# Splitting the next stage's weights piece by piece inside the last block of a two-layer hybrid decoder step, and parting the last two output tiles by columns

## The chip, the cores and the metric

The kernel runs on one core of a Trainium2 chip. The metric is the device time of one execution in microseconds (us), smaller being better. In the profile PE is the matrix engine TensorE, DVE is VectorE, ACT is ScalarE, POOL is GpSimd, and SP is the engine whose queue issues nearly all the transfers here.

## The reference, cut to what matters

The computation is one inference step of a decoder of DEPTH = 2 layers over 2048 prompt rows, 16 meta rows and 8 sample rows, all in fp32, with a width of 1024. Each layer is

```python
proj = einsum('btd,de->bte', rms_norm(h), w_in[l])      # one combined input projection
# its columns are split to four head groups: a (HGRN2), b (gated DeltaNet), c (Mamba-2 SSD), d (retention)
b_conv = causal_conv(b_qkv, gdn_ctx, gdn_conv_w)        # width 4, then silu
c_conv = causal_conv(c_xbc, ssd_ctx, ssd_conv_w, ssd_conv_b)
# each group: a recurrence over chunks of rows, a norm, a gate
y = concatenate([y_a, y_b, y_c, y_d], axis=-1)
h = h + einsum('bte,ed->btd', y, w_out[l])
```

and a last rms_norm follows the second layer. The recurrent states after the prompt and after the samples are outputs too.

## The kernel before

**Tiles and stages.** The 2072 rows are 17 row tiles: tile 0 has 40 rows (meta, samples and padding), the others 128. They make 8 blocks: block 0 is tiles 0 to 2, the others two tiles each. In each layer the kernel runs five stages over all the blocks: C, B, A, D (one head group each: its dense products, convolution, recurrence), then `outproj`, which for each tile multiplies by `w_out`, adds to `h`, stores it, normalizes it and prepares the next layer's input (`xprep`: a row norm, transposes on PE at L518, a high part by ACT at L523 and a low part by DVE at L524, stores to `xh` and `xl`).

**Products.** Each fp32 product is three matmuls over a high and a low part (high by high, low by high, high by low): L484 to L486 for `dense_cm` (columns of the weights on the partitions of the result, up to 296 rows of the block at a time), L494 to L496 for `dense_tm` and `dense_rows` (rows of the block on the partitions). The results land in `pd`, of which there are two buffers.

**Weights.** A piece of weights (128x1024 fp32, 512 KB) is loaded by SP into a buffer `wr` from a pool of five (`f4`), which other tiles share; then ACT casts it to the high part `wh` (L458) and POOL or DVE subtracts that to get the low part `wl` (L459). `wpiece` does all three. Which engine subtracts is set by `lopool[0]`, from the numbers `PC0` (C of layer 0), `PC1` (C of layer 1), `PB`, `PA`, `PD`: 1 is POOL, 0 is DVE, 2 is both in turn. C has row pieces with a small rest `wn` beside (one buffer) and six convolution pieces; B has six convolution pieces (q, k, v in two halves each) and two gate pieces (z); A has eight.

**Order.** The code is written in Python and a scheduler orders the instructions of each engine by a simulated time line; each engine's queue and SP's then run strictly in that order. `early()` raises the priority of what is written inside it. So the weights of the next stage are asked for in one go at its head, in the order that the scheduler finds.

**Convolution.** `conv` (L924) computes six groups of 128 columns. Each takes 24 matmuls into one `pd`, and then four taps: ACT takes the first from `pd` (L953 for C, L955 for B; in block 0 from copies `u`, L943 to L945), DVE adds three (L957) and keeps three columns of history (`hC`, `hB`, L959), ACT takes a tanh (L961) and DVE multiplies (L962). In C, each tile's recurrence begins with PE's `tr<-cc,cb`, and needs `cgu`, which POOL makes by a select (L1417) in a buffer of the W2 pool. POOL's L1534 is a part of the sample rows' recurrence. Beside B's convolution, a chain `walkB` over chunks goes from PE (`wo`, `tr`) through DVE (L313, L1264) and POOL. SP's L1151, L1188 and L1190 belong to its preparation, as do POOL's own transfers `bU` and `bR` (L1161, L1162).

**Between layers.** At tile 16 of layer 0's `outproj`, the next layer's C weights are asked for between its two column halves (`between`).

Of the kernel before, what the change touches and what calls it, by code (L numbers as in the profile page):

```python
# [93 lines left out]
def body(tc, ctx, a, o, nch, depth, blks, off):  # L94
# [87 lines left out]
    PC0, PC1, PB, PA, PD, PO = 1, 1, 1, 2, 0, 0  # L182
# [8 lines left out]
    WEARLY = 1  # L191
# [246 lines left out]
    def wpiece(src, nd, n, wide=False):  # L438
        raw = f4([128, 1024], "wr")
        hi, lo = (wp.tile([128, 4 * 268 if wide else 1024], F32R, tag=("v" if wide else "w") + x, bufs=2 if wide else 6,  # L440
                          name="w" + x) for x in "hl")
        hv, lv = (x[:, 0:nd * n].rearrange("p (d e) -> p d e", d=nd) for x in (hi, lo))
# [5 lines left out]
        for s in src:  # L448
            w = s.shape[1]
            r, c0, c1 = parts[c >= m]  # L450
            nc.sync.dma_start(r.rearrange("p (d e) -> p d e", d=nd)[:, :, c - c0:c - c0 + w],
                              s.rearrange("(o p) e -> p o e", p=128))
            c += w
        on_pool = lopool[0] == 1 or lopool[0] > 1 and (lopool[0] + lopool[1]) % 2
# [5 lines left out]
        return hv, lv  # L460

# [246 lines left out]
    def weightsA(w):  # L708
        return ([load_cm(w, A_Q + 128 * p) for p in range(2)], [load_cm(w, A_F + 128 * p) for p in range(2)],
                load_tm(w, [(A_I, 256)]), [load_cm(w, A_Z + 128 * p, True) for p in range(2)])  # L710

    def mixA(L, W, b):
        wq, wff, wi, wz = W
# [210 lines left out]
    def conv(L, ws, b, wi, key, hasb, out):  # L924
# [10 lines left out]
        for i in range(6):  # L935
# [3 lines left out]
            def ev(ps):  # L939
# [10 lines left out]
                for (src, u0, n, yc) in parts:  # L950
# [60 lines left out]
    def weightsB(w):  # L1011
        return [load_cm(w, B_QKV + 128 * i) for i in range(6)], [load_cm(w, B_Z + 128 * p, True) for p in range(2)]

    def denseB(L, W, b):
        b.qkv = [blk("b" + c) for c in "qkv"]
        conv(L, W[0], b, 0, "B", False, b.qkv)
        z = blk("z")
        for p in range(2):
            dense_cm(W[1][p], b, lambda ps: silu2(ps, z[:, p, 0:b.n], b.n))
            hook(rB)  # L1020
        nc.sync.dma_start(zdr[b.i], z[:, :, 0:b.n])
# [375 lines left out]
    def mixC(L, W, b):  # L1397
# [25 lines left out]
        conv(L, W[1], b, 6, "C", True, xbc)  # L1423
# [238 lines left out]
    def outproj(L, W, t, Ln, between=None):  # L1662
# [3 lines left out]
        yh, yl = xpair((NT - t) % 2, 128)  # L1666
# [4 lines left out]
        for qd in range(2):  # L1671
# [3 lines left out]
            if between:  # L1675
                with early():
                    next(between)
                    Wn = next(between)
        if Ln is not None:
            nc.sync.dma_start(hdr[t], hx[0:R])  # L1680
            xprep(Ln, t, hx)
            if between:
                return Wn
        else:
# [3 lines left out]
            else:  # L1688
                nc.sync.dma_start(o["y_prompt"][0, 128 * (t - 1):128 * t, :], hx)

# [19 lines left out]
    nblk = len(blocks)  # L1710
    ld = load_layer(0)
    Ln = next(ld)
    for l in range(depth):
# [24 lines left out]
        walk.append(walkB(L))  # L1738
        for i in range(-1, nblk, 2):
            bs = blocks[max(i, 0):i + 2]  # L1740
            for b in bs:
                if not b.last:
                    load_x(blocks[b.i + 1])
                denseB(L, W, b)
# [6 lines left out]
            if WEARLY and bs[-1].last:  # L1751
                lopool[0] = PA
                with early():
                    W = weightsA(w)
# [11 lines left out]
        for weights, mix in ((weightsA, mixA), (weightsD, mixD)):  # L1766
            if not (WEARLY and weights is weightsA):
# [80 lines left out]
```

## Time and profile before

| | |
|---|---|
| time, median of 3 runs (lowest to highest) | 2859.1 us (2859.03 to 2863.05) |
| the profiled execution: time, span | 2864.64 us, 2862.9 us |
| mean granted TensorE clock | 0.982 of full |
| busy: PE, DVE, ACT, POOL | 95%, 60%, 36%, 37% |
| stages, layer 0 (ends, about) | C 328, B 614, A 1050, D 1255, outproj 1462 us |
| stages, layer 1 (ends, about) | C 1746, B 2021, A 2455, D 2660, outproj 2863 us |

The profile records for every instruction its start, its duration and, in brackets, how long its engine stood idle before it and what ended that. Times count from the start of the span. The granted clock is a share of 2.4 GHz, so that 0.5 is 1.2 GHz. A mean of 0.8 in a stretch means that the lower level held for 0.4 of it.

### The profile page before, as it was taken

To read this page: it belongs to the slowest core of one execution; us is meant where nothing else is said; L and a number is where in the kernel's file an instruction comes from. 1 tells how busy PE (TensorE), PEld (TensorE's weight loads), DVE (VectorE), ACT (ScalarE), POOL (GpSimd) and SP (SyncE) were. 2 spreads that over 40 slices of the span, in tenths; PEclk is the share of its full clock that TensorE was granted. 3 is DMA by queue.
4 is the path that set the end of the run, shared out by engine and by line. 5 is a ranking of instruction groups with operands and counts; after the bars stand their busy time and mean duration, and the time that the engine had idled before them with its cause. 6 is when DMAs were issued, how large, how long until landed. Compare 5 with 4: busy or idle time off the path is not lost.

```text
span 2862.9 us, 66636 instructions
## 1 busy us (share of the span) xinstructions
PE 2713.3 (95%) x26372; PEld 2463.7 (86%) x26372; DVE 1704.0 (60%) x4864; ACT 1034.1 (36%) x2601; POOL 1065.6 (37%) x2032
## 2 busy tenths in 40 slices
PE   6999999989999899999989999999999999999998
PEld 6889898989889788888778999888898887888787
DVE  5777765657656655454346767656676667445533
ACT  4545532333434422232244445223443443222321
POOL 4454545557323221110033535555773322211100
PEclk9999999999999999999999999999999999999999
DMA  7243445563321423236672433544632323331443
GB/s 179 67 142 110 147 128 139 149 173 102 98 74 61 150 77 113 77 112 204 211 231 80 127 108 119 141 121 134 184 82 90 88 83 114 98 108 67 139 140 111
DMA packets 385152, 349.31 MB, mean 122 GB/s; under 512 B 144312, under 2 KB 349616, under 8 KB 374600
## 3 DMA queue, kind: packets, MB, share of 16 engines
q1 hardware_dynamic: 381320, 335.95, 38.8%
q0 software_dynamic: 3520, 9.09, 1.7%
q8 instruction: 209, 3.42, 0.5%
q14 instruction: 103, 0.84, 0.1%
HBM read 247.05 MB, written 98.10 MB: 121 GB/s over the span
## 4 chain that ended last, share of the span: by engine, by line
PE 74%; DVE 8%; DMA 7%; POOL 4%; ACT 3%; issue 3%; SPq 1%; POOLq 0%; ACTq 0%; DVEq 0%
PE pd L494 10%; PE pd L496 9%; PE pd L495 9%; PE pd L484 9%; PE pd L485 8%; PE pd L486 8%; PE tr L236 7%; PE wo L236 4%; PE sc L236 4%; PE o L236 3%; DMA wr<-in_w_in_dram 3%; PE tr L622 1%; ACT wh L458 1%; PE tr L518 1%; POOL bR L1168 1%
## 5 line engine op out<-in xcount | busy, mean ns | idle before, releaser
L484 PE MATMUL pd<-xh,wh 128*128 128x256 f32 (+1 forms) x2816 | 828.4, 294 | 34.7 <-DVE hB L959 11.5
L486 PE MATMUL pd<-xh,wl 128*128 128x256 f32 (+1 forms) x2816 | 814.8, 289 | 0.6 <-DVE wl L459 0.6
L485 PE MATMUL pd<-xl,wh 128*128 128x256 f32 (+1 forms) x2816 | 815.3, 290 | 0.0
L484 PEld LDWEIGHTS pd<-xh,wh 128*128 128x128 f32 x2816 | 542.7, 193 | 56.9 <-issue 20.0
L494 PE MATMUL pd<-wh,xh 128*128 128x512 f32 (+5 forms) x1632 | 563.1, 346 | 7.4 <-DVE sraw L1406 4.4
L495 PE MATMUL pd<-wl,xh 128*128 128x512 f32 (+5 forms) x1632 | 558.2, 342 | 5.1 <-POOL wl L459 4.4
L496 PE MATMUL pd<-wh,xl 128*128 128x512 f32 (+5 forms) x1632 | 558.2, 342 | 0.0
L486 PEld LDWEIGHTS pd<-xh,wl 128*128 128x128 f32 x2816 | 542.8, 193 | 5.2 <-issue 3.2
L485 PEld LDWEIGHTS pd<-xl,wh 128*128 128x128 f32 x2816 | 542.9, 193 | 3.1 <-issue 1.3
L494 PEld LDWEIGHTS pd<-wh,xh 128*128 128x128 f32 (+1 forms) x1632 | 304.1, 186 | 45.7 <-issue 4.6
L495 PEld LDWEIGHTS pd<-wl,xh 128*128 128x128 f32 (+1 forms) x1632 | 304.4, 187 | 41.6 <-POOL wl L459 5.0
L496 PEld LDWEIGHTS pd<-wh,xl 128*128 128x128 f32 (+1 forms) x1632 | 304.0, 186 | 38.6 <-issue 1.7
L313 DVE TENSOR_TENSOR sbd<-low,tr 64x128 f32<-64x128 f32 x384 | 109.0, 284 | 130.0 <-PE tr L236 116.1
L336 POOL TENSOR_TENSOR fm<-fm,expo 128x4 f32<-128x4 f32 (+3 forms) x136 | 131.1, 964 | 80.0 <-DVE fm L613 72.6
L611 POOL TENSOR_SCALAR fm<-fm 128x4 f32<-128x4 f32 (+3 forms) x102 | 25.0, 245 | 352.1 <-DVE fm L608 325.4
L340 POOL TENSOR_SCALAR rm<-rm 128x1 f32<-128x1 f32 (+1 forms) x51 | 14.0, 275 | 353.5 <-ACT junk L358 352.5
L244 POOL COPY bwi<-wz 32x256 f32<-32x256 f32 x128 | 59.8, 467 | 206.7 <-DVE wz L1264 203.7
L531 ACT ACTIVATE th<-pd 128x256 f32<-128x256 f32 (+2 forms) x162 | 62.5, 386 | 187.4 <-PE pd L486 143.5
L1168 POOL TENSOR_TENSOR bR<-bR,bW 128x120 f32<-128x120 f32 (+14 forms) x300 | 119.0, 397 | 21.0
L1167 POOL TENSOR_TENSOR bW<-bU,bR 128x120 f32<-128x120 f32 (+14 forms) x300 | 112.8, 376 | 33.2 <-DMA bR<-bscr 12.8
L1674 DVE TENSOR_TENSOR hx<-hx,pd 128x512 f32<-128x512 f32 (+1 forms) x68 | 46.6, 686 | 119.9 <-PE pd L496 118.5
L513 DVE SCALAR_TENSOR_TENSOR hx<-hx,rm,sq 128x512 f32<-128x512 f32 (+1 forms) x68 | 53.1, 819 | 104.5 <-POOL rm L336 103.5
(531 smaller groups left out, 5135.6 us busy)
## 6 DMA issues: line engine op xcount, KB each, us to landing
xh<-xh SPq DMA_DIRECT2D x56, 1024.0 KB
xl<-xl SPq DMA_DIRECT2D x56, 1024.0 KB
wr<-in_w_in_dram SPq DMA_DIRECT2D x64, 512.0 KB
hx<-in_x_prompt_dram SPq DMA_DIRECT2D x32, 512.0 KB
y<-y SPq DMA_DIRECT2D x128, 128.0 KB
yf<-y SPq DMA_DIRECT2D x32, 512.0 KB
bld<-qkv SPq DMA_DIRECT2D x32, 384.0 KB
xh<-xh SPq DMA_DIRECT2D x8, 1184.0 KB
```

Source lines behind the costliest of these rows:

```text
L236: T.matmul(out, l, r, start=start, stop=stop, skip_group_check=True)
L313: tt(new[rr, :, hh], low[rr, :, hh], pv, ALU.add)
L336: G.tensor_tensor(dst, src, e.broadcast_to(list(src.shape)), ALU.pow)
L484: T.matmul(ps, hi[:, d], b.xh[:, d, 0:b.n], start=(d == 0), stop=False)
L485: T.matmul(ps, hi[:, d], b.xl[:, d, 0:b.n], start=False, stop=False)
L486: T.matmul(ps, lo[:, d], b.xh[:, d, 0:b.n], start=False, stop=(d == 7))
L494: T.matmul(ps[0:R, 0:n], xh[:, d], hi, start=(d == 0), stop=False)
L495: T.matmul(ps[0:R, 0:n], xh[:, d], lo, start=False, stop=False)
L496: T.matmul(ps[0:R, 0:n], xl[:, d], hi, start=False, stop=(d == 7))
L531: act(th[0:R, 0:n], ps, AF.Tanh, scale=0.5)
L1167: f(wv, bcm(U_[0:2 * nu, j, j + 1:32], 1, m), bcl(R_[0:2 * nu, 0:m, j], 31 - j), ALU.mult)
L1168: f(R_[0:2 * nu, 0:m, j + 1:32], R_[0:2 * nu, 0:m, j + 1:32], wv, ALU.subtract)
```

## The change

1. `PC0` and `PC1` become 0: the low parts of C's weights are computed by DVE and no longer by POOL, in both layers.
2. `wpiece` is parted into `wraw` (the transfer) and `wsplit` (cast and subtract). A generator `staged` keeps transfers two pieces ahead and does one split for each `next`, kept in written order on ACT, DVE and POOL.
3. In the last block of C, B's weights are fed so: one `next` after each of the six groups of `conv`. In the last block of B, A's are, after each of the six groups and the two gate products. `arrived` does what is left.
4. In layer 0's first block of C only the first two convolution pieces are asked for ahead; the other four come one by one inside `conv` (`more`).
5. `outproj` becomes a generator. Between the layers tiles 15 and 16 are done by column halves: both tiles' first half, C's row pieces, both tiles' second half, C's other pieces. Their row end (the store of `h` and `xprep`) is put off until after block 0 of the next layer's C (`tails`).
6. `cgu` of tile 0 moves from the W2 pool to an own small buffer (the tag `bma`).

```diff
-    PC0, PC1, PB, PA, PD, PO = 1, 1, 1, 2, 0, 0
+    PC0, PC1, PB, PA, PD, PO = 0, 0, 1, 2, 0, 0
...
+    def staged(pieces):
+        raws, out = [], []
+        for k, pc in enumerate(pieces):
+            while len(raws) < min(k + 2, len(pieces)):
+                raws.append(wraw(*pieces[len(raws)][0:3]))
+            yield None
+            with inorder((ET.Activation, ET.DVE, ET.Pool)):
+                out.append(wsplit(raws[k], *pc[1:]))
+        yield out
+    coming = []
+    def feed():
+        if coming:
+            coming[1] = next(coming[0], None) or coming[1]
+    def arrived():
+        while coming[1] is None:
+            feed()
+        out = coming[1]
+        coming.clear()
+        return out
...
-    def conv(L, ws, b, wi, key, hasb, out):
+    def conv(L, ws, b, wi, key, hasb, out, more=None):
...
+            if more:
+                with inorder((ET.Activation, ET.DVE)):
+                    next(more, 0)
             dense_cm(ws[i], b, ev, True)
             hook(rB)
+            if b.last:
+                feed()
...
-                gu = w2([128, 4, 128], "cgu", F32R)
+                gu = w2([128, 4, 128], "cgu", F32R) if t else k2.tile([128, 4, 32], F32R, tag="bma", bufs=2, name="cgu")
...
-            W = list(weightsC(w))[-1]
+            more = weightsC(w)
+            W = [next(more) for _ in range(2)][-1]
...
         for b in blocks:
             if not b.last:
                 nextx(blocks[b.i + 1])
-            mixC(L, W, b)
-            if not b.first:
+            else:
+                lopool[0] = PB
+                coming[:] = weightsB(w), None
+            mixC(L, W, b, more if l == 0 and b.first else None)
+            if b.first:
+                for x in tails:
+                    next(x)
+            else:
                 decode(L)
         decode(L, True)
-        lopool[0] = PB
-        with early():
-            W = weightsB(w)
         load_x(blocks[0])
+        W = arrived()
...
+                else:
+                    lopool[0] = PA
+                    coming[:] = weightsA(w), None
                 denseB(L, W, b)
...
-            if WEARLY and bs[-1].last:
-                lopool[0] = PA
-                with early():
-                    W = weightsA(w)
+            if bs[-1].last:
+                W = arrived()
...
-        for t in range(NT):
-            if t == NT - 1 and Ln is not None:
-                lopool[0] = PC1
-                parts = weightsC(a["w_in"][l + 1])
-                W = outproj(L, W, t, Ln, parts)
-            else:
-                outproj(L, W, t, Ln)
+        tails = []
+        for t in range(NT if Ln is None else NT - 2):
+            for _ in outproj(L, W, t, Ln):
+                pass
+        if Ln is not None:
+            lopool[0] = PC1
+            parts = weightsC(a["w_in"][l + 1])
+            both = xpair(1, 256)
+            tails = [outproj(L, W, NT - 2 + k, Ln, [x[:, :, 128 * k:128 * k + 128] for x in both]) for k in range(2)]
+            for _ in range(2):
+                for x in tails:
+                    next(x)
+                with early():
+                    next(parts)
+                    W = next(parts)
```

The lines after it have other numbers: L449 is before's L451, L463 is L458, L991 is L955, L997 is L961, L1460 is L1417, L1577 is L1534.

**POOL between the layers.** In the queue before stand the low parts of C's weights, then the sample rows' L1534, then `cgu`:

```order
L459 TENSOR_TENSOR wl<-wr,wh 128x1024
L459 TENSOR_TENSOR wl<-wn,wh 128x4x12
L336 TENSOR_TENSOR rm<-rm,expo 128x1
L459 TENSOR_TENSOR wl<-wr,wh 128x1024 x4
L340 TENSOR_SCALAR rm<-rm 128x1
L336 TENSOR_TENSOR rm<-rm,expo 128x1
L1765 MEMSET sq_114 128x512
L1765 MEMSET sq_115 128x512
L1534 TENSOR_TENSOR dcS<-dcS,dce 128x1024
L1417 AFFINE_SELECT cgu<-gh 32x4x32 x2
L1417 AFFINE_SELECT cgu<-gh 128x512 x2
```

and now:

```order
L340 TENSOR_SCALAR rm<-rm 128x1
L336 TENSOR_TENSOR rm<-rm,expo 128x1
L1460 AFFINE_SELECT cgu<-gh 32x128 x2
L1577 TENSOR_TENSOR dcS<-dcS,dce 128x1024
L1460 AFFINE_SELECT cgu<-gh 128x512 x2
```

The weights have left this queue, and `cgu` of tile 0 (`32x...`) stands ahead of the sample rows' step, that of tile 1 still behind it.

**ACT where B ends and A begins, layer 1.** `bv` are the last two groups of the last block's convolution (the first piece of a group is L955, its tanh L961), and `wh<-wr` are casts of A's weights. Before:

```order
L961 ACTIVATE th<-bv 128x256
L955 ACTIVATE bv<-pd,cwh 128x256
L961 ACTIVATE th<-bv 128x256
L1273 COPY boq<-wo 32x256
L531 ACTIVATE th<-pd 128x256
L458 CAST wh<-wr 128x1024
```

and now:

```order
L991 ACTIVATE bv<-pd,cwh 128x256
L1316 COPY boq<-wo 32x256
L463 CAST wh<-wr 128x1024
L997 ACTIVATE th<-bv 128x256
L463 CAST wh<-wr 128x1024 x2
L991 ACTIVATE bv<-pd,cwh 128x256
L306 ACTIVATE low<-sbd_113,bEG 128x128 x2
```

Three casts stand ahead of the last group's first tap, where none did. In layer 0 two casts stood there before (L458 x2 ahead of the second L955), and three do now.

**SP at the start of layer 0.** `wr<-in_w_in_dram 128x8x128` is a convolution piece of C, `hx` an input tile, `xh_135` the store of the prepared block 0. Before:

```order
L451 DMA wr<-in_w_in_dram 128x8x128
L380 DMA cwt<-in_gdn_conv_w_dram 128x6x1
L382 DMA cwt<-in_ssd_conv_w_dram 128x6x1
L387 DMA cb<-in_ssd_conv_b_dram 128x6x1
L451 DMA wr<-in_w_in_dram 128x8x128 x2
L1699 DMA xh_135<-xh 128x2368
L1699 DMA xl_143<-xl 128x2368
```

and now:

```order
L1739 DMA xh_135<-xh 128x2368
L395 DMA smc<-in_ssd_d_dram 128x4
L405 DMA lg<-in_hgrn_lb_logits_dram 128x2x1
L1739 DMA xl_143<-xl 128x2368
L405 DMA lg<-in_hgrn_lb_logits_dram 128x2x1
L350 DMA hx<-in_x_prompt_dram 128x1024 x2
L970 DMA cx<-in_state_ssd_conv_dram 24x256 x3
L449 DMA wr<-in_w_in_dram 128x8x128 x3
```

Three of the six convolution pieces have moved behind the stores of block 0 and two input tiles of block 1; the sixth comes later still.

## Rows read from the trace of the kernel before

**Rows 1.** The page, part 1: busy time, share of the span, instructions.
```profile
PE 2713.3 (95%) x26372; PEld 2463.7 (86%) x26372; DVE 1704.0 (60%) x4864; ACT 1034.1 (36%) x2601; POOL 1065.6 (37%) x2032
```

**Rows 2.** Table by stretch; the last three columns are granted clock, DMA share, GB/s.
```profile
core 0: us, PE busy (x) PEld busy (x) DVE busy (x) ACT busy (x) POOL busy (x), PEclk, DMA share, GB/s
328.00:340.00 12.00, 7.63 (x46) 7.22 (x45) 9.14 (x20) 3.25 (x13) 6.39 (x5) 0.86 0.25 106
595.00:610.00 15.00, 5.96 (x44) 5.41 (x43) 6.45 (x15) 4.97 (x9) 5.85 (x8) 0.79 0.98 207
1462.50:1519.20 56.70, 42.36 (x269) 40.77 (x267) 30.22 (x87) 26.21 (x68) 21.94 (x18) 0.82 0.67 187
...
1502.00:1505.00 3.00, 3.00 (x24) 3.00 (x23) 2.88 (x8) 1.60 (x5) 0.00 (x0) 1.00 0.11 1
...
2009.00:2032.00 23.00, 21.16 (x309) 20.03 (x302) 11.91 (x33) 10.04 (x21) 11.98 (x17) 1.00 1.05 253
```

**Rows 3.** Timeline of PE between the layers: start, duration, instruction, [idle before, releaser].
```profile
1469.66 0.32 PE L495 MATMUL pd<-wl,xh 128*40 128x268 f32 x1 [2.50 <-POOL wl L459]
...
1492.40 0.62 PE L484 MATMUL pd<-xh,wh 128*128 128x296 f32 x1 [4.65 <-ACT u L945]
...
1512.57 0.31 PE L236 MATMUL sc<-cgu,l128r 32*32 32x128 f32 x1 [5.91 <-POOL cgu L1417]
```

**Rows 4.** Groups by line, 1462.5 to 1519.2 us: busy, mean ns, idle before.
```profile
L513 DVE SCALAR_TENSOR_TENSOR hx<-hx,rm,sq 128x512 f32<-128x512 f32 x4 | 2.8, 750 | 6.8 <-POOL rm L336 6.8
...
L458 ACT CAST wh<-wr 128x1024 fp32r<-128x1024 f32 x6 | 6.2, 1040 | 12.2 <-DMA wr<-in_w_in_dram 12.2
...
L459 POOL TENSOR_TENSOR wl<-wr,wh 128x1024 fp32r<-128x1024 f32 x6 | 14.5, 2418 | 16.5 <-ACT wh L458 16.4
...
L1417 POOL TENSOR_SCALAR_AFFINE_SELECT cgu<-gh 32x128 fp32r<-32x128 f32 (+1 forms) x4 | 2.1, 533 | 14.3 <-DMA xh<-xth 14.1 <-DMA xl<-xtl 0.2
```

**Rows 5.** Timelines of POOL, DVE and PE, layer 0, from C to B.
```profile
324.94 7.24 POOL L459 TENSOR_TENSOR wl<-wr,wh 128x1024 fp32r<-128x1024 f32 x3
...
325.05 2.60 DVE L615 TENSOR_TENSOR on<-coi,fm 128x256 f32<-128x256 f32 x1
...
332.68 0.46 PE L236 MATMUL tr<-cc,cb 128*128 128x128 f32 x2 [3.94 <-DVE cc L962]
```

**Rows 6.** Timelines of ACT and PE, layer 0, from B to A.
```profile
598.62 1.04 ACT L458 CAST wh<-wr 128x1024 fp32r<-128x1024 f32 x1 [5.73 <-DMA wr<-in_w_in_dram]
603.79 1.04 ACT L458 CAST wh<-wr 128x1024 fp32r<-128x1024 f32 x1 [4.13 <-DMA wr<-in_w_in_dram]
604.86 0.47 ACT L955 ACTIVATE bv<-pd,cwh 128x256 f32<-128x256 f32 x1
...
608.97 0.55 PE L484 MATMUL pd<-xh,wh 128*128 128x256 f32 x1 [6.33 <-DVE hB L959]
```

**Rows 7.** Timelines of SP, ACT, DVE and PE, layer 1, from B to A.
```profile
2010.40 1.33 SPq L1193 DMA_DIRECT2D bz<-z  x1
...
2014.31 2.00 SPq L451 DMA_DIRECT2D wr<-in_w_in_dram  x2
...
2013.03 0.47 ACT L955 ACTIVATE bv<-pd,cwh 128x256 f32<-128x256 f32 x1 [0.57 <-DVE pd L948]
...
2019.95 1.05 ACT L458 CAST wh<-wr 128x1024 fp32r<-128x1024 f32 x1 [1.90 <-DMA wr<-in_w_in_dram]
...
2028.17 1.05 ACT L458 CAST wh<-wr 128x1024 fp32r<-128x1024 f32 x1 [4.99 <-DMA wr<-in_w_in_dram]
...
2021.03 1.23 DVE L459 TENSOR_TENSOR wl<-wr,wh 128x1024 fp32r<-128x1024 f32 x1 [1.37 <-ACT wh L458]
...
2018.05 0.36 PE L484 MATMUL pd<-xh,wh 128*128 128x256 f32 x1
```

**Rows 8.** Timelines of ACT and PE at the start of layer 0.
```profile
31.38 1.04 ACT L458 CAST wh<-wr 128x1024 fp32r<-128x1024 f32 x1 [2.61 <-DMA wr<-in_w_in_dram]
...
33.38 0.36 PE L494 MATMUL pd<-wh,xh 128*128 128x268 f32 x1 [4.44 <-DVE sraw L1406]
```

More of the change, by code (lines that the diff above doesn't have):

```diff
@@ L435, in load_layer, with wraw @@
         yield L
-    def wpiece(src, nd, n, wide=False):
+    def wraw(src, nd, n):
         raw = f4([128, 1024], "wr")
-        hi, lo = (wp.tile([128, 4 * 268 if wide else 1024], F32R, tag=("v" if wide else "w") + x, bufs=2 if wide else 6,
-                          name="w" + x) for x in "hl")
-        hv, lv = (x[:, 0:nd * n].rearrange("p (d e) -> p d e", d=nd) for x in (hi, lo))
         m = 1024 // nd
@@ L453, in wpiece, with wsplit @@
             c += w
+        return parts
+    def wsplit(parts, nd, n, wide=False):
+        hi, lo = (wp.tile([128, 4 * 268 if wide else 1024], F32R, tag=("v" if wide else "w") + x, bufs=2 if wide else 6,
+                          name="w" + x) for x in "hl")
+        hv, lv = (x[:, 0:nd * n].rearrange("p (d e) -> p d e", d=nd) for x in (hi, lo))
         on_pool = lopool[0] == 1 or lopool[0] > 1 and (lopool[0] + lopool[1]) % 2
@@ L708, in weightsA @@
     def weightsA(w):
-        return ([load_cm(w, A_Q + 128 * p) for p in range(2)], [load_cm(w, A_F + 128 * p) for p in range(2)],
-                load_tm(w, [(A_I, 256)]), [load_cm(w, A_Z + 128 * p, True) for p in range(2)])
+        return staged([cm_piece(w, A_Q + 128 * i) for i in range(4)]
+                      + [([w[512 * k:512 * k + 512, A_I:A_I + 256]], 4, 256, False) for k in range(2)]
+                      + [cm_piece(w, A_Z + 128 * p, True) for p in range(2)])
     def mixA(L, W, b):
-        wq, wff, wi, wz = W
+        wq, wff, wi, wz = W[0:2], W[2:4], W[4:6], W[6:8]
         q, f, kk = blk("aq"), blk("af"), blk("ak")
@@ L1011, in weightsB @@
     def weightsB(w):
-        return [load_cm(w, B_QKV + 128 * i) for i in range(6)], [load_cm(w, B_Z + 128 * p, True) for p in range(2)]
+        return staged([cm_piece(w, B_QKV + 128 * i) for i in range(6)] + [cm_piece(w, B_Z + 128 * p, True) for p in range(2)])
     def denseB(L, W, b):
         b.qkv = [blk("b" + c) for c in "qkv"]
-        conv(L, W[0], b, 0, "B", False, b.qkv)
+        conv(L, W[0:6], b, 0, "B", False, b.qkv)
         z = blk("z")
         for p in range(2):
-            dense_cm(W[1][p], b, lambda ps: silu2(ps, z[:, p, 0:b.n], b.n))
+            dense_cm(W[6 + p], b, lambda ps: silu2(ps, z[:, p, 0:b.n], b.n))
             hook(rB)
+            if b.last:
+                feed()
         nc.sync.dma_start(zdr[b.i], z[:, :, 0:b.n])
@@ L1395, in weightsC, with mixC @@
         yield W
-    def mixC(L, W, b):
+    def mixC(L, W, b, more=None):
         zc = rowtile(b, "cz")
@@ L1422, in mixC @@
         ahead = [front(b.tiles[0])]
-        conv(L, W[1], b, 6, "C", True, xbc)
+        conv(L, W[1], b, 6, "C", True, xbc, more)
         if b.last:
@@ L1659, in decD, with outproj @@
         finish(0, 3, o0[0:TR0], TR0, EPS, L.wD, z0, L.bD)()
-    def outproj(L, W, t, Ln, between=None):
+    def outproj(L, W, t, Ln, pair_=None):
         R = rows(t)
@@ L1674, in outproj @@
             tt(hx[0:R, cs], hx[0:R, cs], ps, ALU.add)
-            if between:
-                with early():
-                    next(between)
-                    Wn = next(between)
+            yield
         if Ln is not None:
@@ L1681, in outproj @@
             xprep(Ln, t, hx)
-            if between:
-                return Wn
         else:
@@ L1766, in body @@
         for weights, mix in ((weightsA, mixA), (weightsD, mixD)):
-            if not (WEARLY and weights is weightsA):
+            if weights is weightsD:
                 lopool[0] = PD
```

9 lines of the change are left out of this document (7 added, 2 removed).

## The prediction

> **What bounds the kernel now.** I read the page first: PE is busy 95% of the span, DVE 60%, ACT and POOL under 40% [rows 1]. So a change pays only where PE stands still or runs at its lower clock, 1.2 GHz. The dense work itself isn't touched by this change: no matmul is added or taken away. Next I listed PE's pauses over 0.4 us. They are few, and the long ones lie where a stage hands over to the next, which is where the change works. Then a table of those stretches gives for each what it holds against what it needs at full clock [rows 2]. I take PE's busy time times its granted clock as the need:
>
> - between the layers (from the last `outproj` product to `tr<-cc,cb` of tile 0): 42.36 x 0.82 = 34.7 us needed, 56.7 spent, 22 lost;
> - from B to A in layer 0: 5.96 x 0.79 = 4.7 needed of 15.0, 10 lost; in layer 1 the stretch of 23.0 us has PE busy 21.16 at full clock, under 2 lost;
> - from C to B in layer 0: 7.63 x 0.86 = 6.6 of 12.0, 5 lost. In layer 1 no pause there reaches 1 us;
> - the start of layer 0: one pause of 4.44 us behind an eviction [rows 8], others that belong to the first loads of x and aren't touched.
>
> Last I asked for each of them what the waiting instruction waits for, and where the new order puts that.
>
> **Between the layers: +13 (6 to 19).** Three pauses are named [rows 3]. 2.50 us wait for a low part on POOL, which takes 2.42 us for each of six pieces [rows 4]. 4.65 wait for ACT's copy of a `pd`. 5.91 wait for POOL's `cgu`, and POOL itself stood 14.1 us in all before it for stores `xh<-xth` to release a W2 buffer [rows 4]: the row end of tile 16. With 14.3 us or so of idle time in the stretch, the remaining 7 to 8 are the lower clock that follows the pauses.
>
> The change takes each cause away. The row ends of tiles 15 and 16 come after block 0; `cgu` of tile 0 has its own buffer, and stands ahead of L1534 on POOL; row pieces are asked for a half tile earlier, so that the cast's 12.2 us of waiting for transfers [rows 4] falls mostly beside `outproj`; the low parts go to DVE. Six at 1.23 us [rows 7] are 7.4 us more for DVE, in a stretch where it has 30.22 [rows 2], of which the row ends' L513 has 2.8 [rows 4] and L524 about as much, and leave. What is left is some 24.7, nearly all of it six groups' taps, 4.1 us a group. That is more than a group's PE work: 24 matmuls, which take 3.0 us at full clock [rows 2]. So DVE takes over as the bound: row pieces, three times as many matmuls, 9 us, first group 3.0, then 24.7 plus about four low parts, 4.9, makes 42 us, less the few taps of the last group that `tr<-cc,cb` doesn't wait for: some 40 to 41. Against 56.7 that is 16 saved, and 1 more from the pause at the last `outproj` half. The put-off transposes of two tiles come back, by my estimate as 2 us of PE, and their DVE work as 1. `cgu` of tile 1 still waits behind L1534, whose operand comes by a chain of transfers: 0 to 3, I take 1. So +13. The low end is DVE's bound with a pause of 3.4 us and the lower clock behind it; the high end is PE at its need, 34.7, less 2.
>
> POOL and DVE hold each other up: DVE's L615 took 2.60 us, from 325.05 on, beside a low part of 2.41 on POOL that began at 324.94, and both end at about the same time [rows 5]. The Trainium skill (SBUF — State Buffer, "Who interferes with whom") states as a rule that VectorE and GpSimd share one pair of ports and that the one that holds it shuts the other out. This trace agrees. By that rule the low parts on DVE would now hold POOL's `cgu` 1.2 us each time, and the sum of this part would be 12.
>
> **The start of layer 0: +1 (-4 to +6).** The eviction before the 4.44 us pause sat on ACT behind a cast that waited 2.61 us for its transfer [rows 8]. That cast is now later on ACT, so the pause goes, and low parts of 2.4 us become 1.2. But four of six pieces are now requested behind the stores of block 0 and two tiles of x, 3.4 MB ahead of them in all. At the 207 to 253 GB/s that transfers reach in stretches where their share is full [rows 2] that is some 15 us, and PE, which starts its groups some 4 to 6 us sooner, has two groups and a tile's transposes to spend meanwhile. So groups 2 and on wait, and the gain is mostly paid back. The low end is a wait as long as that pause; the high one is that pause and its clock.
>
> **C to B.** Layer 0: +1 (-2 to +5). The 3.94 us before `tr<-cc,cb` come from three low parts in a row on POOL, 7.24 us, which hold DVE's taps [rows 5]. `PB` stays 1, so those low parts stay on POOL; only their places change, and two groups of B now stand ahead of that transpose as cover. The ends are the loss of the stretch, 5, and a wait of a low part more, 2. Layer 1: -2 (-6 to 0). There the low parts stood apart from each other and cost nothing; now five stand almost in a row with `cgu` of the last tiles behind them, which is the pattern of layer 0. Its 5 us, and 1 more, are the low end.
>
> **B to A.** Here casts wait for transfers at the head of ACT, and the last group's first tap is queued behind them. Layer 0 shows the price: casts that waited 5.73 and 4.13 us, L955 behind them at 604.86, and PE's next product waiting 6.33 us for the `pd` [rows 6]. In the new order not two but three casts stand ahead of that tap, with the request to SP only one transfer (`bld`) earlier. So I take +1 (-2 to +10): the third cast and its transfer against some 1.5 us of earlier landing; the high end is the loss of the stretch.
>
> Layer 1 had its tap ahead of the casts, at 2013.03, and PE went on to its next group at 2018.05 without a pause [rows 7]. Now three casts stand ahead of it. The requests go out behind SP's L1193, so at about 2011.7 and not 2014.31 [rows 7]. The first cast waited until 2019.95, 5.6 us after its request, the third until 2028.17 [rows 7]; with the small transfers behind and not before them, I put the third landing at about 2019 to 2020. The tap then starts at 2021, three DVE taps and a low part or two follow, and `pd` is free at 2023: 5 us after PE wants it at 2018.05. So -5 (-12 to 0), the low end being layer 0's loss of 10 with a third cast.
>
> **The sum.** 13 + 1 + 1 - 2 + 1 - 5 = 9 us. All else (`staged` itself, the tanh tables, layer 1's last `outproj`) issues the same instructions, and PE is there the bound without pauses. The profiled execution took 2864.64 us, of which the span is 2862.9; so 2855.6 in its terms, and 2850 against the median of 2859.1, which is 5.5 lower.
>
> **The rivals.** (a) *The transfers two ahead cover all.* The pieces land before their casts come up, the pauses of layer 0 go (5 and 10) and layer 1 gets none: 14 + 1 + 5 + 10 = 30, so 2829. For it: the transfers are independent of all else. Against it: SP's queue in the new order holds them back, and 5.6 us of landing are longer than a group. The Trainium skill (DMA: Bandwidth & Descriptors, "Rules for kernel authors") has this as its advice, to issue early and wait late; layer 0's rows, where a wait of 5.73 us stands on ACT, show that the early issue isn't there. Chance 0.10.
>
> (b) *Splits ahead of taps.* Slower. The cast that waits at the head of ACT, kept in written order, holds the taps in all four fed blocks: B to A -12 in layer 1 and -5 in layer 0 (one cast more), C to B -5 in layer 1 and -3 in layer 0. With 13 + 1 it is -11, so 2870. It decides from the point where the third piece lands over 12 us after its request, as one did [rows 7]. Chance 0.13.
>
> (c) *DVE eats the gain between the layers.* Its 4.1 us a group and the low parts, with the put-off row ends in block 1, leave 5 of the 13, and the hand-overs take 5: 2859. Chance 0.17.
>
> (d) *The order undoes the feeding.* Landings, not splits, set the hand-overs, as before, and nothing changes there, in layer 1 neither: 13 + 1, so 2845. Chance 0.15.
>
> **How the numbers follow.** The forecast has 0.45, with 2844 to 2856 of its own. 0.2% is 5.7 us, about what a measurement of this kernel can tell from no change. Faster by more (under 2853.4): most of the forecast (0.38), (a) and (d), 0.63. Same: the rest of it and most of (c), 0.22. Slower: (b) and a little of (c), 0.15. The range leaves out (a) and most of (b): 2836 to 2866.
>
> **What would show it.** Between the layers, the stretch from the end of `outproj` to `tr<-cc,cb` at 40 to 43 us, DVE near 90% busy in it, no pause before `sc<-cgu` over 2 us. In B to A of layer 1, a new pause of about 5 us before `pd L484`, released by the copy `hB` of the last tap, with ACT's casts waiting for `wr` just ahead; in layer 0 the old one, about as long. From C to B in layer 0 a pause of 1 to 3 us. At the start, the 4.44 gone and a new wait for a piece in the third group or after. The forecast is wrong if the stretch between the layers stays over 48 us, if layer 1's B to A has no pause (then it is faster, toward 2845), or if its pause is over 8.

## The result: 2894.5 us, 35 us slower

| | before | after |
|---|---|---|
| median (lowest to highest) | 2859.15 us | 2894.47 us (2890.66 to 2897.86) |
| ratio, 95% interval | | 1.0124 (1.0107 to 1.0140) |
| profiled execution: time, span | 2864.64, 2862.9 us | 2896.26, 2894.6 us |
| mean granted TensorE clock | 0.982 | 0.974 |

The forecast was 2850 with a range of 2836 to 2866, and 0.63 for faster. The result lies outside the range, beyond the slowest rival (2870).

The first part of the page after, to be held against [rows 1]:

```profile
PE 2724.4 (94%) x26372; PEld 2472.2 (85%) x26372; DVE 1716.4 (59%) x4884; ACT 1038.1 (36%) x2601; POOL 1020.2 (35%) x2012
```

The span grew by 31.7 us. PE does the same 26372 matmuls and is busy 11.1 us longer, since more of them run at the lower clock (mean granted clock 0.974 against 0.982); the other 20.6 us are idle time of PE (170.2 us of the span against 149.6). So about two thirds of the loss are pauses, and one third is what the clock takes behind them.

To see where it lies, I matched PE's matmuls of the two traces by line and number, and took how much later each starts after the change. Read where both kernels have the same order again, that lag gives the ledger (plus is a gain). Inside B of layer 1 the order differs and the lag goes up and down between some 23 and 35 us, so that the parting of the last two losses there is rough.

| stretch | lag goes from, to | gain | predicted |
|---|---|---|---|
| start of layer 0 (to 105 us) | 0 to 5.7 | -5.7 | +1 |
| C to B and early B, layer 0 | 5.7 to 23.4 | -17.7 | +1 |
| B to A, layer 0 | 23.4 to 21.7 | +1.7 | +1 |
| A and D, layer 0 | 21.7 to 18.5 | +3 | 0 |
| between the layers, with the row ends put off | 18.5 to 6.9 | +11.6 | +13 |
| C to B and early B, layer 1 | 6.9 to 26.6 | -19.7 | -2 |
| B to A, layer 1 | 26.6 to 33.0 | -6.4 | -5 |
| the rest | 33.0 to 31.6 | +1.4 | 0 |

Four terms came out near the size that was forecast (the section on the prediction says which of them for its own reason). The loss lies where C hands over to B, in both layers, and a smaller one at the start. PE's rows of layer 0 there, from the timeline of the kernel after (start, duration, instruction, idle time before it and what ended that):

```profile
361.77 0.69 PE L657 MATMUL tr<-ident,on 128*128 128x128 f32 x2 [7.24 <-DVE on L650]
366.75 0.32 PE L657 MATMUL tr<-ident,on 40*128 40x40 f32 x1 [4.29 <-DVE on L650]
...
369.40 0.61 PE L519 MATMUL pd<-xh,wh 128*128 128x296 f32 x1 [0.16 <-ACT wh L463]
```

and of layer 1:

```profile
1782.82 0.69 PE L657 MATMUL tr<-ident,on 128*128 128x128 f32 x2 [5.28 <-DVE on L650]
1787.78 0.32 PE L657 MATMUL tr<-ident,on 40*128 40x40 f32 x1 [4.28 <-DVE on L650]
```

The pause of 3.94 us that stood there before [rows 5] is gone. In its place PE waits for `on`, the normed result of C's last tiles, 7.24 and 4.29 us, in a chain that goes from PE through ACT, POOL and DVE. That chain is hardly longer than before: from `coi<-wo,eg` on DVE to `on` it takes 5.75 us for the full tile against 4.69, and from `coi<-o,cz` to `on` 2.27 us for the tile of 40 rows against 2.22. What is missing is the work that used to lie beside it. In the kernel before (where L484 is L519 here, and L622 is L657) B's dense products fill this time, and PE goes from them to the same transpose without a pause:

```profile
355.10 0.38 PE L484 MATMUL pd<-xh,wh 128*128 128x296 f32 x1
...
362.96 0.38 PE L622 MATMUL tr<-ident,on 128*128 128x128 f32 x2
```

A table of these stretches (busy time of each engine, then granted clock) shows what the pauses do to the clock, 0.79 and 0.68. At C's last transposes in the kernel before, from 344 to 370 and from 1760 to 1785 us, it is 1.00, with PE busy 26.00 of 26 and 24.52 of 25 us. After the change:

```profile
344.00:384.00 40.00, 27.40 (x189) 24.45 (x188) 20.00 (x73) 17.63 (x66) 15.77 (x17) 0.79 0.17 40
...
1768.00:1800.00 32.00, 19.41 (x112) 15.96 (x111) 14.38 (x48) 13.03 (x48) 15.27 (x17) 0.68 0.11 30
```

Why the cover is missing is in ACT's, POOL's and SP's rows of layer 0:

```profile
334.63 1.03 ACT L463 CAST wh<-wr 128x1024 fp32r<-128x1024 f32 x1
...
362.55 0.63 ACT L1550 ACTIVATE y<-tr,pv 128x128 f32<-128x128 f32 x2 [2.37 <-issue]
...
367.93 0.48 ACT L1550 ACTIVATE y<-tr,pv 128x40 f32<-128x40 f32 x2
368.30 2.93 ACT L463 CAST wh<-wr 128x1024 fp32r<-128x1024 f32 x3
...
369.42 7.06 POOL L464 TENSOR_TENSOR wl<-wr,wh 128x1024 fp32r<-128x1024 f32 x3 [3.18 <-ACT wh L463]
...
330.40 1.17 SPq L449 DMA_DIRECT2D wr<-in_w_in_dram  x1
```

B has eight pieces, and `conv` calls `feed` six times. The first call only asks for transfers, so the six calls make five splits. The other three are made by `arrived`, which the program calls after `decode(L, True)`, the tail of the sample rows; `inorder` keeps them behind what is written ahead of them. So the last three casts stand on ACT right behind `y<-tr,pv 128x40`, the tail's last row, 33 us after the fifth cast and 38 after the last transfer was issued. Three groups of B (v's second half and both z, about 3.3 us each) can't start before that. In the kernel before, all eight casts were done at 325 us, and those groups ran beside C's tail.

### The profile page after: what moved, and what is told of

The parts are those of the page before. It is cut to its first block, busy times and chain, and to the rows that moved or that the text cites. A ratio compares the mean times of both kernels' runs of the same rounds, so it can differ in the third digit from the quotient of the medians.

```text
span 2894.6 us, 66654 instructions
## 1 busy us (share of the span) xinstructions
PE 2724.4 (94%) x26372; PEld 2472.2 (85%) x26372; DVE 1716.4 (59%) x4884; ACT 1038.1 (36%) x2601; POOL 1020.2 (35%) x2012
## 5 line engine op out<-in xcount | busy, mean ns | idle before, releaser
L519 PE MATMUL pd<-xh,wh 128*128 128x256 f32 (+1 forms) x2816 | 835.2, 297 | 41.6 <-DVE hB L995 24.5
L519 PEld LDWEIGHTS pd<-xh,wh 128*128 128x128 f32 x2816 | 546.7, 194 | 64.3 <-issue 26.5
L306 ACT ACTIVATE low<-sbd,bEG 128x128 f32<-128x128 f32 x256 | 88.6, 394 | 68.6 <-DVE sbd L313 68.4
```

Of the source, the lines that this page charges most:

```text
L306: S.mul(low[:, p], old[:, p], decay(p))
L519: T.matmul(ps, hi[:, d], b.xh[:, d, 0:b.n], start=(d == 0), stop=False)
```

## The experiments

All are small edits of the kernel before or after. They were run in five sittings on four chips, each beside the kernel before, whose median lay between 2857.1 and 2859.4; the ratio is to the kernel before of the same sitting, and a difference of medians between sittings can be off by some 2 us. "Pair" names the part between the layers alone (halves, put-off row ends, `PC1` 0, `cgu` in its own buffer), to which other parts are then added one at a time.

| kernel | median us | ratio to before, 95% interval |
|---|---|---|
| E1 after, last splits ahead of the sample tail | 2887.09 | 1.0104 (1.0076 to 1.0133) |
| E2 after, B's weights in one go as before | 2868.24 | 1.0039 (1.0027 to 1.0052) |
| E3 after, A's weights in one go as before | 2893.92 | 1.0130 (1.0109 to 1.0152) |
| E4 the pair | 2848.80 | 0.9972 (0.9958 to 0.9986) |
| E5 E1 with six splits by calls | 2878.65 | 1.0071 (1.0045 to 1.0097) |
| E6 pair and the new start | 2860.82 | 1.0008 (0.9989 to 1.0027) |
| E7 pair and A fed | 2863.21 | 1.0015 (0.9998 to 1.0031) |
| E8 pair and B fed | 2890.43 | 1.0113 (1.0086 to 1.0140) |
| E9 E8, last three splits with priority | 2876.86 | 1.0076 (1.0055 to 1.0098) |
| E10 E8, six splits by calls, last two with priority | 2854.45 | 0.9987 (0.9971 to 1.0003) |
| E11 E10 with `PB` 0 | 2851.79 | 0.9981 (0.9972 to 0.9991) |
| E12 after, B mended as in E10 | 2875.92 | 1.0056 (1.0032 to 1.0080) |
| E13 E7, A split from z's groups on | 2838.11 | 0.9932 (0.9908 to 0.9955) |
| E14 E12 with the old start | 2864.40 | 1.0022 (1.0009 to 1.0034) |
| E15 E14, A split as in E13 | 2863.63 | 1.0018 (1.0002 to 1.0035) |
| E16 E13 once more | 2838.88 | 0.9933 (0.9908 to 0.9957) |

**Undoing one part of the change.** E1 moves one line:

```diff
+        W = arrived()
         decode(L, True)
         load_x(blocks[0])
-        W = arrived()
```

> The changed kernel with one edit: what is left of B's splits (arrived) is written ahead of the sample rows' tail (decode(L, True)) instead of behind it. Theory 1: the loss from C to B comes from the three last splits, which stand on ACT behind that tail, so that PE has no dense work; then the pauses of 7.24 and 4.29 us in layer 0 and of 5.28 and 4.28 in layer 1 go, the lower clock behind them too, and the time falls from 2894 by some 30 us to about 2863. Theory 2: POOL's low parts in a row hold DVE's taps, as the prediction had it; then the order of the last splits matters little and the time stays above 2885.

Measured 2887.1, 7 us less than after (the two intervals overlap), where theory 1 expected some 30. The trace says why: the three casts moved ahead of the tail's last `y`, and in place of the 4.29 us there are 1.70, but they still stand behind the `y` of C's last full tile, and the first pause is there as before.

```profile
362.06 0.63 ACT L1550 ACTIVATE y<-tr,pv 128x128 f32<-128x128 f32 x2 [2.37 <-issue]
362.58 2.93 ACT L463 CAST wh<-wr 128x1024 fp32r<-128x1024 f32 x3
```

So the size of my theory was wrong, not yet its kind: the edit moved the casts by 6 us, and some 40 were wanted.

E2 and E3 put B's or A's weights back to one request in one go:

```diff
-                coming[:] = weightsB(w), None
...
-        W = arrived()
+        lopool[0] = PB
+        with early():
+            W = [wpiece(*pc) for pc in ...]
```

> The changed kernel with B's weights asked for in one go at B's head, as before; all else of the change stays. Theory 1: everything that is lost from C to B (17 and 20 us in the two traces) comes back, so about 2857. A rival: the loss there comes from the put-off row ends or from DVE's low parts in C; then under 10 us come back and the time stays above 2884.

> The changed kernel with A's weights asked for in one go, as before. Theory: the pause of 9.35 us from B to A of layer 1 goes, which the traces show as 6 us of lag, and layer 0 gets back its old pause, which is as long as the new one: about 2888. Rival, feeding A is harmless and the lag there is a leftover of the late start of B: no change, 2894.

B's feeding is worth 26 us of the loss, and A's none, on top of the rest. In E3's trace, with A unfed, PE still stands 8.51 us where A begins in layer 0 and 5.91 in layer 1: its rival had the time right.

**One part alone.** E4 is the pair: before, with part 5 of the change, and of parts 1 and 6 what goes with it. E6 adds the start, E7 and E8 the feeding of A or of B, each with the lines of the change:

```diff
# E4, against before
-    PC0, PC1, PB, PA, PD, PO = 1, 1, 1, 2, 0, 0
+    PC0, PC1, PB, PA, PD, PO = 1, 0, 1, 2, 0, 0
# E6, against E4 (PC0 is 0 there too)
-            W = list(more)[-1]
+            W = [next(more) for _ in range(2)][-1]
# E7 and E8, against E4
+                    coming[:] = weightsA(w), None
+                coming[:] = weightsB(w), None
```

> The kernel before with the part between the layers alone: last two tiles by column halves, row ends put off, cgu in its own buffer, low parts of layer 1's C weights on DVE. Theory: this part gains what the lag of the two traces shows there, 11 to 12 us net, so about 2847. Rival: the gain is paid back in layer 1's first blocks, or the halves make layer 0's end slower: 2855 or more.

> The part between the layers (2848.8 alone) and the new start of layer 0 (low parts on DVE, four pieces one by one inside conv), nothing fed ahead. By the lag of the traces the start loses 4 to 6 us: about 2854. The prediction had +1 gained there: 2848.

> The part between the layers and A's weights fed in the last block of B; start and B's weights as before. By the lag of the traces from B to A layer 1 loses 6 to 7 us and layer 0 gains 1 to 2: about 2853. Rival: as undoing it in the changed kernel gave nothing back, no change from 2849.

> The part between the layers and B's weights fed in the last block of C; start and A's weights as before. Undoing it in the changed kernel gave 26 us back, so adding it should cost about as much: 2870 to 2875. If it costs far less, the loss needs another part beside it (the start's or A's).

The pair is faster than before by 9 us (the prediction had 13). The start costs 12 by the medians, 5.2 by the lag in the trace; A costs 14, where the two terms of the prediction from B to A make a loss of 4; B costs 42. These don't add up with E2 and E3: 9 - 12 - 14 - 42 would be 59 slower, and it is 35. E8's trace has the pauses of the changed kernel again:

```profile
354.16 0.69 PE L657 MATMUL tr<-ident,on 128*128 128x128 f32 x2 [7.24 <-DVE on L650]
359.12 0.33 PE L657 MATMUL tr<-ident,on 40*128 40x40 f32 x1 [4.28 <-DVE on L650]
```

**Moving B's last casts far enough.** E5 is E1 with one more `feed()` where the pieces are set, so that six splits come from the calls. E9 is E8 with `early()` in place of `inorder` for what `arrived` splits. E10 has both and E1's line too; E11 is E10 with B's low parts on DVE.

```diff
                 coming[:] = weightsB(w), None
+                feed()
...
-            with inorder((ET.Activation, ET.DVE, ET.Pool)):
+            with (early() if rest[0] else inorder((ET.Activation, ET.DVE, ET.Pool))):
# E11, against E10
-    PC0, PC1, PB, PA, PD, PO = 1, 0, 1, 2, 0, 0
+    PC0, PC1, PB, PA, PD, PO = 1, 0, 0, 2, 0, 0
```

> The changed kernel with two edits for B: the first transfers are asked for ahead of the last block of C, so that the six feeds there split six pieces and not five, and what is left (the two gate pieces) is written ahead of the sample rows' tail. Theory 1 (PE lacks dense work while C's tail runs, because the pieces of B's last groups are split behind it): the sixth group's 3.3 us move into the pause of 7.2 us at tr<-on in both layers, so some 4 to 8 us under the 2887 of the kernel with the second edit alone: about 2880. A rival, that feeding itself holds up C's last block: no gain over 2887.

> The kernel before with the part between the layers and with B fed piece by piece (the same as the run before it of that pair, 2890.4 us, whose trace stands 41 us behind the pair's kernel without feeding), but the pieces that are still whole when all are asked for are split ahead in priority, not kept behind the sample rows' tail: their three casts then stand about 30 rows of ScalarE earlier, ahead of the last tile's fsq and y. Theory 1 (the three casts' place behind y is the cost): both pauses at tr<-ident,on of each layer go (7.24 + 4.28 and 5.49 + 4.27 us) with the half clock behind them (some 17 us at half rate, about 8 us each), so 2890 - 37 + what is late next = 2855 to 2866. Rival (the five fed splits themselves slow C's last tile, wherever the other three stand): the 7 us pauses stay, and the time is 2880 or more.

> As the run ahead of it, and one more call when the pieces are set, so that six are split by the calls inside C and two are left; these are asked for ahead of the sample rows' tail and in priority. Theory 1: as the run ahead of it or up to 5 us less, 2850 to 2865. Rival (fed splits in C's last tile are the cost): as slow or slower than the run ahead of it. If the pauses at tr<-on are gone but the 8 us at tr<-ident,bld is still there, that pause is no consequence of the casts' lateness.

> As the run ahead of it, but B's low halves are made on VectorE (1.2 to 2.0 us each) and not on GpSimd (2.4 us each, 19.5 us in all). Theory 2 (GpSimd's low halves push back B's first solve, and with it the pause of 8 us at tr<-ident,bld): that pause goes and the time falls by 8 to 15 us in both layers together. Rival (the solve is late because of what comes ahead of it on TensorE and VectorE, or because its gathers share the DMA engines with the loads of xh and xl): the pause stays, and the time is the same or, with VectorE now holding 10 us more work in C's last tile, up to 10 us longer.

E5's time came as expected, but the first pause hardly shrank (6.99 us): its last two casts stood behind that `y` too. In E9 and E10 ACT makes all eight casts by 335 us, and neither kernel has a pause before `tr<-ident,on`. E10 is at 2854.5: of B's 42 us, 36 are gone. E9, which has its last cast as early (333.64 us against 333.93), took off only 14, so the casts' place explains the two pauses but not all of the 36. ACT's last three casts in E10, and the stretch of C's last tiles, where 27 of 40 us busy at a clock of 0.79 in E8 (340 to 380 us) are now 45 of 50 at full clock:

```profile
327.45 1.03 ACT L463 CAST wh<-wr 128x1024 fp32r<-128x1024 f32 x1
...
329.86 1.03 ACT L463 CAST wh<-wr 128x1024 fp32r<-128x1024 f32 x1
...
333.93 1.03 ACT L463 CAST wh<-wr 128x1024 fp32r<-128x1024 f32 x1
...
318.00:368.00 50.00, 45.01 (x355) 43.53 (x354) 40.86 (x102) 23.00 (x77) 26.80 (x26) 1.00 0.43 129
```

The pause of some 8 us before `tr<-ident,bld`, which the changed kernel has where B's first solve ends,

```profile
465.04 0.37 PE L1255 MATMUL tr<-ident,bld 128*32 128x128 f32 x1 [8.59 <-DMA bld<-qkv]
```

is not at that place in E9 to E11. Theory 2 (GpSimd's low parts push the solve back) falls: E10 has them on GpSimd without that pause, and E11, with them on DVE, can't be told from it by its time. A shorter one stands nearby in E10, 4.00 and 6.05 us before `tr<-tb,bke` in the two layers, released by POOL; E11 has 2.53 us there in layer 0 and none over 1.5 us in layer 1, so that a smaller part for GpSimd stays open. Whether the late casts cause the pause of 8 us stays open too, since kernels with B in one go have such a pause as well, 7.4 us in E4 and 7.9 in E13, both in layer 1. E9 stays at 2876.9. Its lag against the pair is back at 2 us at 440 us of layer 0, then grows to 14 over B's second half, and again in layer 1; which step does that I haven't settled. Against E10 it has a new pause of 6.15 us before a product of B at 340.67 us, released by ACT's `u`, where E10 has 1.42 us at most. Of the 27 us between the two traces at the end 7 stand at 400 us of layer 0, and 9 come in A of layer 0, which neither edit touches.

**The full change with B mended, and A.** E12 and E14 are the changed kernel with E10's three edits, E14 with the old start (E6's lines undone). E13 takes A's first splits out of v's groups; E15 does the same in E14.

```diff
-            if b.last:
+            if b.last and key == "C":
                 feed()
...
                     coming[:] = weightsA(w), None
+                    feed()
```

> The changed kernel whole (start, B and A fed, the part between the layers), with B's feeding mended as in the run of 2854.4 us: one more call when the pieces are set, and what is left asked for ahead of the sample rows' tail and in priority. Theory 1 (the place of B's last three casts is the step that failed): the changed kernel's 2894.5 us loses what mending took off the pair's kernel (2890.4 to 2854.4, 36 us), so 2858, and 2855 to 2868 with what A and the start still cost. Rival (in the full change the loss has further causes of its own, in the start and in A, that show as soon as B's is gone, and add up as they did alone: 12 and 14 us): 2875 to 2882.

> As the first run of these three, but with layer 0's start as it was in the kernel before (all six pieces of C split ahead in one go). If the start costs what the traces of the pair said (5.2 to 5.7 us), 4 to 7 us less than the first run. Rival (the prediction's +1, and the 12 us between medians that lie some 10 us apart in their own runs was scatter): within 3 us of it.

> The pair between the layers and A fed (2863.2 us; its trace has TensorE idle 9.37 us in layer 1, while ScalarE's first cast of A waits 7.56 us for its transfer with v's two evictions behind it), but no piece of A is split inside v's groups: the first splits come with z's two groups. Theory 3 (a cast whose transfer has not landed, placed ahead of v's evictions, holds them up): the 9.37 us falls under 5, and the time to 2850 to 2856. Rival (A's transfers are late and the casts would be waited for wherever they stand): the pause stays or moves to A's first group, and the time is 2860 or more.

E12's rival had the time right: mending B took 19 us off the changed kernel, not 36. E14 against E12 puts the start at 11.5 us, as E6 did, so those 12 us weren't scatter alone. And E13 is 25 us faster than E7, 10 faster than the pair, and the fastest kernel of all: its interval (0.9908 to 0.9955) lies below the pair's (0.9958 to 0.9986). ACT in E7, layer 1, where B ends (casts of A and the tap of v's last group):

```profile
2004.65 1.04 ACT L463 CAST wh<-wr 128x1024 fp32r<-128x1024 f32 x1 [7.56 <-DMA wr<-in_w_in_dram]
2008.09 1.04 ACT L463 CAST wh<-wr 128x1024 fp32r<-128x1024 f32 x1 [2.40 <-DMA wr<-in_w_in_dram]
2009.88 1.05 ACT L463 CAST wh<-wr 128x1024 fp32r<-128x1024 f32 x1 [0.75 <-DMA wr<-in_w_in_dram]
2010.84 0.47 ACT L991 ACTIVATE bv<-pd,cwh 128x256 f32<-128x256 f32 x1
```

and in E13:

```profile
1985.94 0.47 ACT L991 ACTIVATE bv<-pd,cwh 128x256 f32<-128x256 f32 x1 [0.57 <-DVE pd L984]
...
1991.39 1.05 ACT L463 CAST wh<-wr 128x1024 fp32r<-128x1024 f32 x1 [0.41 <-DMA wr<-in_w_in_dram]
```

In E7 the tap of v's last group stands behind three casts that wait 10.7 us for transfers. DVE waits for the casts too: its low parts, kept in order, stand ahead of `wz`, and it is `wz` that releases PE after 9.37 us of idle time:

```profile
2010.96 1.70 DVE L464 TENSOR_TENSOR wl<-wr,wh 128x1024 fp32r<-128x1024 f32 x1 [3.60 <-ACT wh L463]
2012.59 0.40 DVE L1307 TENSOR_TENSOR wz<-bwi,wo 32x256 f32<-32x256 f32 x1
...
2013.05 1.22 PE L236 MATMUL tr<-wz,bkt 128*128 128x128 f32 x4 [9.37 <-DVE wz L1307]
```

In E13 the tap is done before the first cast. The edit moved a second thing, though: the extra call lets SP issue the first two transfers at 1986.66 and not at 1995.19, so E13 doesn't part the casts' place from the transfers' time, nor the tap on ACT from the low parts on DVE.

> The part between the layers, B's feeding mended, and A's first splits taken out of v's groups: the run of 2864.4 us with the one edit that took 25 us off the pair's kernel with A (2863.2 to 2838.1). Theory 3 (that edit mends A whether or not B is fed): 2864 - 25 = 2839, 2836 to 2846. Rival (with B fed, A's pause comes from B being late, as where A was unfed in the changed kernel and the pause stayed): 2855 or more.

> The pair's kernel with A's first splits taken out of v's groups once more, beside the run ahead of it on one chip, since the two lie nearer to each other than executions of one kernel scatter: 2836 to 2842. If B's mended feeding costs its 5 us of the pair here too, the run ahead of it is 4 to 8 us longer; if it is worth something once A is mended, it is shorter.

E16 repeats E13 beside E15: 2838.9 against 2863.6. So the edit that gave 25 us without B's feeding gives 1 with it, and the rival had the time right. PE's rows in E15, layer 1, where A begins:

```profile
2005.12 0.61 PE L522 MATMUL pd<-xh,wh 128*128 128x296 f32 x1 [4.89 <-ACT wh L463]
2008.91 0.62 PE L522 MATMUL pd<-xh,wh 128*128 128x296 f32 x1 [2.08 <-ACT wh L463]
```

With B fed, C's hand-over is quicker for the dense products: E15's lead E16's by 7 to 13 us at 430 to 505 us of layer 0, while most rows of `walkB` there come up to 17 us later, since the order differs. But in layer 1 A's first two transfers go out at 1997.02 against 1986.17, and ACT's casts wait 16.1 us in all for A's transfers, against 7.4 in E16 (in layer 0, 17.2 against 3.9). From 620 us on all rows lag, at first by 7 to 8 us: what the dense products had gained is gone after the hand-over from B to A. By the end the lag is 22. Why A's requests move by 10 us when B is fed, and where E15 loses the rest of the 25, stays open.

## Why the prediction was wrong, step by step

**C to B: the step that failed.** The prediction said that in the new order "two groups of B now stand ahead of that transpose as cover", and priced layer 0 at +1 and layer 1 at -2. The cover at `tr<-cc,cb` was real, the 3.94 us are gone (E4, without B's feeding, has 4.48 us there, E8 none). But I counted only what was fed ahead, and didn't ask where the pieces that are not fed go. Six calls make five splits; three of eight come after the program's next section. The cover of C's tail was three groups of B, and the change took it away. In the order of ACT's instructions the casts stand behind `y 128x40`, so it could have been read before any run. The terms were -17.7 and -19.7. Shown by E8 (the part alone brings the pauses, and 42 us) and by E9 and E10: both have the casts ahead of C's tail and neither has the pauses. What the casts' place is worth by itself is less sure: 14 us of the 42 went in E9, 36 in E10, which has a sixth split by calls and E1's line as well.

**The start: mis-sized.** Expected were +1 and -4 at the low end; the lag in the trace is -5.7, and E6 and E14 have -12 by the medians. The mechanism came in the main as said: the pause of 4.44 us [rows 8] is gone, PE is 4.2 us ahead at about 38 us, and then loses it to late pieces. No row of PE waits for a piece itself; but `xl` and `u`, for which PE stands 2.46 and 1.70 us, come behind the last cast. The last cast waits longer for its transfer than any in the start of the kernel before, where 2.61 us was the longest:

```profile
53.66 1.05 ACT L463 CAST wh<-wr 128x1024 fp32r<-128x1024 f32 x1 [4.80 <-DMA wr<-in_w_in_dram]
```

Not foreseen were the smaller pauses that come with it (2.98 us for a low part, where 1.43 stood, and 2.44 before the transposes of the next tile), and the clock, at a mean of 0.87 from 15 to 110 us against 0.94 before (15 to 105 us). The price differs from execution to execution: at 200 to 290 us the seven traces with the new start lie 3.8 to 11.2 us behind the kernel before, the ten with the old start between 3.4 us ahead of it and 0.8 behind. The means of the two groups are some 8 us apart, an estimate from these traces, between the 5.7 us of the changed kernel's own trace and the 12 of the medians.

**Between the layers: right in size, by luck.** +11.6 against +13. From the last `outproj` product to `tr<-cc,cb` it is 45.8 us, not 40 to 43, so that the stretch gave 11 us and not 16:

```profile
1474.20:1520.00 45.80, 39.11 (x263) 37.05 (x262) 29.02 (x88) 21.89 (x60) 4.13 (x5) 0.93 0.54 154
```

I held that DVE would take over as the bound, near 90% busy. It is at 63%; PE at 85% sets the pace, with two pauses of over 2 us: 2.84 us for `cgu` of tile 1, which I had at 1, and 2.19 us for ACT's `u`. Of the three causes named in [rows 3] the low part and `cgu` of tile 0 are gone; `u` is halved, from 4.65 us. Two more terms made up for the stretch. By the lag of the products, layer 0's `outproj` gained 6 us ahead of it (18.5 to 12.6), which I didn't have, and the row ends that were put off cost 6 behind it (1.2 to 6.9), where I had 3. E4, the pair alone, shows the same three parts: 5, 11 and -6. Why `outproj` gains is not shown.

**B to A: the pause was foreseen, but not its size, and its cause is only in part the one I gave.** Layer 1 was to get a new pause of about 5 us before its next product, released by `hB`, with casts waiting just ahead. It is there at 9.35 us, past the 8 that the prediction named as a sign of being wrong; the lag grew by 6.4 against -5. Layer 0 has 8.30 us where 6.33 stood, and gained 1.7. Layer 1's row:

```profile
2054.90 0.55 PE L519 MATMUL pd<-xh,wh 128*128 128x256 f32 x1 [9.35 <-DVE hB L995]
```

E13 shows a cure where B is in one go. E3 and E8 show that the term isn't independent of C to B: without A's feeding, but with B late, PE stands at that hand-over too, in E8 7.32 us before the same product. So how much of the 9.35 us comes from A's feeding is not shown.

**The sum and the rivals.** Rival (b), splits ahead of taps, had the sign, and casts do stand ahead of the tap in B to A; its C to B part (-8) stood for the wrong mechanism. The true one wasn't among the rivals: I listed rivals on what the change does to the pieces it feeds, and none on the pieces it leaves. Rival (a) said that transfers asked for early cover all. The Trainium skill (DMA: Bandwidth & Descriptors, "Rules for kernel authors") advises to issue early and wait late. Here transfers were early, the last issued at 330.40, and the wait had gone to another place: a cast that stood in a queue until 368. By the Trainium skill (PSUM — Partial Sum Buffer, "Engine vs sequencer instructions") the queues of ScalarE, VectorE and GpSimd are strictly first in, first out. The trace agrees: the first of the three casts began at 368.30, as the row ahead of it (from 367.93, 0.48 us long) came to its end.

## What to carry to other kernels

When preparation is spread over the steps of a stage, count the calls against the pieces, and find the place in each engine's order where the remainder lands: the pieces that weren't fed cost more here than the fed ones gained. Ask of every piece what it covers for, not only what it waits for, since the work that hides another stage's tail is seen in no row of waits. And put a step whose operand comes by a transfer behind the short steps that share its queue, not ahead of them: with earlier requests beside it, that took 25 us off E7, though only 1 off E14.

## What the runs showed that I had not expected

Executions of one kernel scatter more than the three runs of before showed (2859.03 to 2863.05): over 19 runs on one chip they lie between 2849.3 and 2863.8. The profiled executions of E4 and E6, which differ in the start alone, are 5 us apart where the medians are 12 apart. Terms of a few us can be read from a trace's lag, but the scatter of one execution has to be kept in mind beside it.

The parts of the change don't add up: alone on the pair A costs 14 and B 42, undone from the whole they give back 0 and 26, and A's mended form is worth 25 us without B's feeding and 1 with it. In E15 a hand-over that came early found the next one's transfers late; whether the one brings the other is open.

The two pauses of C to B in layer 0, 11.5 us, are not all that the hand-over cost: the lag went from 0.3 us ahead of the kernel before to 18.3 behind it. Another pause of 2.42 us at 398.59 belongs to that, and the clock, which stood at its lower level of 1.2 GHz in and behind the pauses: the mean of 0.79 over 40 us means for 17 of them, in layer 1 the mean of 0.68 over 32 us for 20.
